# One layer of a hybrid streaming encoder on one core: four joint stores in the tail, halved last casts, and the places of four other steps

## The chip, the cores and the metric

The kernel runs on one core of one Trainium2 chip. The core's engines are TensorE (PE in the profile, its weight loads apart as PEld), VectorE (DVE), ScalarE (ACT), GpSimd (POOL) and SyncE (SP). Each runs its own list of instructions in order and waits for the others by semaphores. DMAs are issued from an engine's list and are carried out beside it. The metric is the device time of one execution in microseconds (us).

## The reference

The input `x` is 512 tokens by 2048 channels, everything is float32. One layer computes two branches from the same normalised input, merges them, and adds a gated embedding:

```python
h = rmsnorm(x, g_pre)
qkv, z_a, b_raw, a_raw, glu_in, z_b, gate_logits = split(h @ w_in)
# A: short convolution, 16 heads of 128, chunks of 64 tokens, a gated delta rule
#    with a triangular solve in each chunk and a state carried over the chunks
o_a = rmsnorm(gated_delta_chunked(q, k, v, g_log, beta), g_dn_out) * silu(z_a)
y_a = o_a @ w_br_a
# B: gated linear unit, depthwise convolution of 31 taps, layer norm
u = silu(layernorm(depthwise(glu(glu_in)) + b_dw)) * silu(z_b)
y_b = u @ w_br_b
mixed = (gate_a * y_a + gate_b * y_b) @ w_out
x = x + rmsnorm(mixed, g_post)
e = p @ w_ple_proj                                  # 256 channels to 2048
x = x + rmsnorm(sigmoid(x @ w_ple_gate) * e, g_ple)
```

`rmsnorm` divides by the root of a mean over all 2048 channels of a token, so the last line needs a token's whole row of gate products before any of it can be scaled.

## The kernel before, in words

**Products.** Every float32 product is made of three TensorE products: both operands are split into a high part (a cast, on ScalarE) and a low part (the difference, on VectorE or GpSimd), and high by high, high by low and low by high are added up in PSUM. A piece of weights is 128 by 1024; its load (SP), its cast and its subtraction run ahead of TensorE by a few pieces. The usual product is 128 by 128 by 512.

**Order of work.** Python code issues the work in one order; a scheduler then orders each engine's list by a model of when inputs are ready, with the issue order as priority. `pin` (keep_in_program_order) keeps an instruction behind the one that was issued before it on its engine. Side work is written as generators: `spawn` starts one, every big product calls `tick`, and a generator that yields n continues n ticks later. `finish` runs what is left without any products in between.

**Start.** `load_x` loads and normalises the four token tiles and, between them, computes the embedding `e`: `embed` (L221) runs for each of four column blocks j, with four PSUM banks (`e_ps`, out of six), one a token tile. For each half k of the 256 channels and each token tile it issues high by high (L228), high by low weights (L229) and low by high (L230). The results are copied (`e_sb`) by ScalarE and VectorE in turn and stored to `pe_dram` by POOL (L507).

**Heads.** The products by `w_in` (L183 to L187) follow; `group(g)`, eight of them with two heads each, runs among them by ticks. A group transposes k, q and v, computes the Gram products `pg` (L862) of all chunks and a product with a swap matrix that exchanges the halves of the squared norms (L869, `pe`), then solves the triangular systems: 31 steps on VectorE (L898, L899), one after the other, each followed by a yield of as many ticks as its size times `pace`, 2.6. The last transpose of the result (`Tc`, L913) is followed by a yield of 22 ticks and by the products `py` and `pz` (L919, L922) and `pd` (L934). Then two `head_scan` run over the chunks, ending in a norm, a product with z and four transposes (`po`, L797). The last group, g = 7, has no group behind it: its scans end in `finish("heads")`.

**Middle.** Branch B, the two products by `w_br_a` and `w_br_b`, and `w_out` follow. `presums` lets POOL's DMAs add up blocks of weights in DRAM, for products that use seven block products in the place of eight; its queue work lies beside the heads.

**End.** The gate product is made of 14 block products (`PLAN`): P1, P2, P3, P6, P7, Q4, Q5 for two column blocks jp. LOW are token tiles 0 and 1, HIGH are 2 and 3. `next_piece_sw` (L1620) keeps up to four split pieces ahead: `split_piece` (L1602) casts a whole piece, 1024 wide, into a buffer of `ring` or `s3` (L1616) and subtracts (L1617). There are 112 pieces in all; the last four, 108 to 111, are those of the last block product, Q4 of jp 1. After each piece's products `step` (L1905) issues up to three `chores` and up to two `scalings`. Chores of a finished product add blocks (L1960), take a sigmoid (L1950), multiply by e and square (L1951, L1953), and multiply by the gain (L1956).

`with_x` (L1723) forms x1, x plus the normalised branch output. For LOW it also stores x1 to the output (L1727), since for these tiles the last sum is made in DRAM: when LOW's gated embedding is complete, `final_steps` (L1967) takes the mean of squares (L1574, L1575) and its power of -1/2 (POOL, L1577), and for each column block j scales on ScalarE (L1973) and adds to the output with an accumulating DMA of POOL (L1974). Eight such DMAs go out, 256 KB each, 128 rows of 2 KB. For HIGH the last sum is one VectorE instruction (L1976) and a plain store by SP (L1977).

After the last product come, in the order of issue: the third tile's mean and power, the additions for the fourth tile in two halves (L2045), the third's first final step, then the fourth's sigmoid and products alternating with the third's steps, the fourth's mean and power, and the rest of the final steps.

Of the kernel before, what the change touches and what calls it, by code (L numbers as in the profile page):

```python
# [81 lines left out]
def _body(ctx, tc, A, out):  # L82
# [138 lines left out]
    def embed(j, pT, xps):  # L221
        ps = [xps.tile([P, T], F32, tag="xp", name="e_ps") for _ in range(NTT)]
        for k in range(2):
            wh, wl = prepped.popleft()
            lh, ll = pT[k]
            for tt in range(NTT):
                b = slice(tt * P, (tt + 1) * P)
                mm(ps[tt], lh[:, b], wh, start=k == 0, stop=False)  # L228
                mm(ps[tt], lh[:, b], wl, start=False, stop=False)  # L229
                mm(ps[tt], ll[:, b], wh, start=False, stop=k == 1)  # L230
        for tt in range(NTT):
            e = slots.tile([P, T], F32, tag="s", name="e_sb")
            (nc.vector.tensor_copy if tt % 2 else nc.scalar.copy)(e, ps[tt])
            e_sb[j, tt] = e
# [572 lines left out]
    def group(g):  # L807
# [48 lines left out]
        for hh, h, s4, kq, kc, vc in heads:  # L856
            pg = wps.tile([P, NTT, 2, 64], F32, tag="w", name="pg")
            for c in range(8):
                tt, par = divmod(c, 2)
                a = 64 * par  # L860
                pair = kq[:, tt, 0:2, :] if par == 0 else kq[:, tt, 3:1:-1, :]
                mm(pg[a:a + 64, tt, :, :], kq[:, tt, 3 * par, :], pair, start=True, stop=True)  # L862
            pgs.append(pg)
        yield 6
# [3 lines left out]
        pe = wps.tile([P, T], F32, tag="w", name="pe")  # L868
        mm(pe[:, 0:8], cc(C_SWAP), sq, start=True, stop=True)  # L869
# [21 lines left out]
        owed, pace = 0.0, 2.6  # L891
# [22 lines left out]
        yield 22  # L914
# [686 lines left out]

    def split_piece():  # L1602
# [3 lines left out]
        two = []  # L1606
        for m in range(2):
# [12 lines left out]
    def next_piece_sw():  # L1620
        while entries and len(sources) < (3 if entries[0][0] is GATE else 5):
            load(*entries.popleft())
        while len(pieces) < (3 if count[0] < 10 else 4) and sources:
            split_piece()
            if entries and len(sources) < (3 if entries[0][0] is GATE else 5):
                load(*entries.popleft())
        return pieces.popleft()

    def mms(ps, pr, piece, q, t, opnd=None):
        wh, wl = piece  # L1630
        for n in range(2):
            kk = 2 * q + n
            c = slice(n * T, n * T + T)
            lh, ll = (opnd or mix_opnd)(OPND[pr], kk, t)
            mm(ps, lh, wh[:, c], start=kk == 0, stop=False)  # L1635
            mm(ps, ll, wh[:, c], start=False, stop=False)  # L1636
            mm(ps, lh, wl[:, c], start=False, stop=kk == 7)  # L1637
# [82 lines left out]
    def x_steps(tts, xr):  # L1720
        rm = inv_rms(ssm[:, tts[0]:tts[0] + 2, :], f"m{tts[0]}")

        def with_x(j):  # L1723
            for n, tt in enumerate(tts):
                pin(nc.vector.scalar_tensor_tensor(x1[tt][j], x1[tt][j], rm[:, n:n + 1], xr.pop((tt, j)), ALU.mult, ALU.add))
                if tt in LOW:
                    nc.gpsimd.dma_start(rows(out, tt, j), x1[tt][j])  # L1727
# [177 lines left out]
    def step():  # L1905
# [5 lines left out]
        for _ in range(2):  # L1911
            if scalings:
                scalings.popleft()()
# [16 lines left out]
    e_t = {}  # L1930
    grow = [None] * 4

    def load_e(tts, j, home=None):
        if home:
            two = [unit(home, "e") for _ in tts]
        else:
            w = s3.tile([P, 1024], F32, tag="rw", name="ew", bufs=5)
            two = [w[:, 0:T], w[:, T:]]
        for tt, e in zip(tts, two):
# [27 lines left out]
    def final_steps(tt, width=4):  # L1967
        rp = inv_rms(ssp[:, tt:tt + 1, 0:width], f"p{tt}")

        def one(j):  # L1970
            e = e_t[tt, j]
            if tt in LOW:
                pin(nc.scalar.activation(e, e, AF.Copy, scale=rp))  # L1973
                pin(nc.gpsimd.dma_start(rows(out, tt, j), e, accum_op=ALU.add))  # L1974
                return
            pin(nc.vector.scalar_tensor_tensor(e, e, rp, x1[tt][j], ALU.mult, ALU.add))  # L1976
            nc.sync.dma_start(rows(out, tt, j), e)  # L1977
        return [lambda j=j: one(j) for j in range(4)]

    v = {}  # L1980
    for pr, jp in PLAN[:-1]:
# [25 lines left out]
        elif pr == "P3":  # L2007
# [4 lines left out]
            if jp:  # L2012
                chores.append(lambda: scalings.extend(final_steps(0) + final_steps(1)))
# [28 lines left out]
    third = final_steps(2)  # L2042
    for h in range(2):
        cs = slice(h * 256, h * 256 + 256)
        pin(nc.vector.tensor_tensor(u[1][:, cs], ps[1][:, cs], u[1][:, cs], ALU.add))  # L2045
    third[0]()
    for h in range(2):
        halves_[h][0]()
        third[1 + h]()
    for h in range(2):  # L2050
        halves_[h][1]()
    fourth = final_steps(3, 5)
    third[3]()
    for f in fourth:
        f()
# [65 lines left out]
```

## Time and profile before

| | |
|---|---|
| time, median of 3 runs | 2391.76 us (2390.85 to 2392.19) |
| profiled execution | 2392.39 us |
| its span | 2390.6 us |
| TensorE busy in it | 2366.1 us |
| VectorE busy | 1905.8 us |
| ScalarE busy | 1235.1 us |
| GpSimd busy | 560.4 us |
| TensorE's granted clock, mean | 0.998 of full speed |

Times within the profile count from the start of the span. A row of the timeline has the start, the duration (of several instructions together where xN stands behind), the engine, the line of the kernel, the operation, the tiles out<-in with their shape, and in brackets the idle time of the engine before it and what ended it. An engine followed by q (SPq) is its sequencer. A row of waits has who waited for whom, the total in us, how often, and the longest. A row of windows has the stretch, its length, then for PE, PEld, DVE, ACT and POOL the busy time with the number of instructions in brackets, the granted clock, the DMA share and GB/s. A row "DMA to landing" has the shortest, the median and the longest time from issue to the last byte.

### The profile page before, as it was taken

What the parts mean: (1) busy time and instruction counts of PE and PEld (TensorE: products, weight loads), DVE (VectorE), ACT (ScalarE), POOL (GpSimd) and SP (SyncE); (2) the same over time, 40 slices, a digit from 0 to 9 for tenths busy, and PEclk for the clock granted to TensorE, in tenths of its full rate; (3) what the DMA queues carried; (4) which work ended last, traced back from release to release, by engine and by line L of the source; (5) the groups of instructions that cost most, each with busy time, mean ns of one, the idle gap of its engine ahead of it and who ended that gap; (6) DMA issues with size and microseconds to landing.
All of it is one profiled execution on the core that took longest, in us unless ns stands there. A gap on an engine that the chain in (4) does not pass through costs nothing.

```text
span 2390.6 us, 33765 instructions
## 1 busy us (share of the span) xinstructions
PE 2366.1 (99%) x11774; PEld 1949.3 (82%) x11774; DVE 1905.8 (80%) x3509; ACT 1235.1 (52%) x2413; POOL 560.4 (23%) x607
## 2 busy tenths in 40 slices
PE   9999999999999999999999999999999999999997
PEld 7888888887888888888888887888888888888786
DVE  8878888776777786767778677999998898887877
ACT  6455455555644545454544544554423665665655
POOL 1001100011122122231321231798861000000001
PEclk9999999999999999999999999999999999999999
DMA  7577766765486768686874884443353577767666
GB/s 277 164 202 200 200 204 197 205 180 188 146 224 173 209 200 252 175 228 194 220 239 144 214 237 115 148 150 106 115 167 119 186 249 240 258 221 234 214 229 167
DMA packets 152827, 465.67 MB, mean 195 GB/s; under 512 B 17872, under 2 KB 26320, under 8 KB 151120
## 3 DMA queue, kind: packets, MB, share of 16 engines
q1 hardware_dynamic: 121456, 334.00, 41.2%
q0 software_dynamic: 28896, 125.32, 22.6%
q10 hardware_dynamic: 2304, 4.20, 0.6%
q8 instruction: 92, 1.51, 0.3%
q14 instruction: 79, 0.65, 0.1%
HBM read 426.22 MB, written 134.22 MB: 234 GB/s over the span
## 4 chain that ended last, share of the span: by engine, by line
PE 88%; DVE 4%; issue 3%; DMA 2%; ACT 2%; POOL 0%; SPq 0%; POOLq 0%; DVEq 0%; ACTq 0%
PE g L185 13%; PE g L187 13%; PE g L183 13%; PE zp L471 6%; PE zp L473 6%; PE zp L472 6%; PE f L1637 4%; PE f L1636 4%; PE f L1635 4%; PE yp L1466 2%; PE yp L1462 2%; PE yp L1464 2%; PE yp L1143 2%; PE yp L1141 2%; PE yp L1139 2%
## 5 line engine op out<-in xcount | busy, mean ns | idle before, releaser
L185 PE MATMUL g<-hl,w 128*128 128x512 f32 x1536 | 610.5, 397 | 0.0
L187 PE MATMUL g<-hh,w 128*128 128x512 f32 x1536 | 608.3, 396 | 0.0
L183 PE MATMUL g<-hh,w 128*128 128x512 f32 x1536 | 608.1, 396 | 0.0
L126 ACT CAST w<-raw 128x512 fp32r<-128x512 f32 x564 | 345.8, 617 | 416.1 <-PE g L187 240.6
L127 DVE TENSOR_TENSOR w<-raw,w 128x512 fp32r<-128x512 f32 x450 | 310.4, 696 | 85.5 <-ACT w L126 83.1
L185 PEld LDWEIGHTS g<-hl,w 128*128 128x128 f32 x1536 | 289.0, 188 | 55.2 <-issue 1.4
L187 PEld LDWEIGHTS g<-hh,w 128*128 128x128 f32 x1536 | 289.1, 188 | 54.1 <-POOL w L127 0.3
L183 PEld LDWEIGHTS g<-hh,w 128*128 128x128 f32 x1536 | 289.1, 188 | 54.0
L1011 DVE SCALAR_TENSOR_TENSOR uc<-up,vec,uc 128x497 f32<-128x497 f32 (+29 forms) x390 | 282.3, 733 | 13.2 <-ACT uc L990 1.9
L127 POOL TENSOR_TENSOR w<-raw,w 128x512 fp32r<-128x512 f32 x114 | 146.5, 1299 | 57.2 <-ACT w L126 55.1
L1635 PE MATMUL f<-wsp,oph 128*128 128x512 f32 x352 | 137.8, 391 | 0.0
L710 DVE SCALAR_TENSOR_TENSOR cv<-g,vec,cv 128x511 f32<-128x511 f32 x144 | 106.6, 740 | 39.1 <-ACT cv L708 38.8
L1636 PE MATMUL f<-wsp,opl 128*128 128x512 f32 x352 | 137.4, 390 | 0.0
L1637 PE MATMUL f<-wsp,oph 128*128 128x512 f32 x352 | 137.2, 390 | 0.0
L1617 DVE TENSOR_TENSOR wsp<-raw,wsp 128x1024 fp32r<-128x1024 f32 x81 | 98.7, 1222 | 34.5 <-ACT wsp L1616 28.9
L1616 ACT CAST wsp<-raw 128x1024 fp32r<-128x1024 f32 x81 | 83.8, 1047 | 64.1 <-PE f L1636 40.7
L1141 PE MATMUL yp<-w,oh 128*128 128x512 f32 x256 | 100.1, 391 | 0.0
L1143 PE MATMUL yp<-w,ol 128*128 128x512 f32 x256 | 99.5, 391 | 0.0
L1139 PE MATMUL yp<-w,oh 128*128 128x512 f32 x256 | 99.1, 389 | 0.0
L898 DVE TENSOR_TENSOR prod<-UT,VT 128x2 f32<-128x2 f32 (+30 forms) x248 | 87.6, 353 | 6.5
L1033 POOL TENSOR_TENSOR uc<-uc,pr 128x511 f32<-128x511 f32 (+29 forms) x60 | 75.9, 1266 | 8.3 <-ACT pr L1032 7.7
L721 POOL COPY kq<-kc 128x512 f32<-128x512 f32 x16 | 11.5, 720 | 282.9 <-issue 150.9
(438 smaller groups left out, 4947.4 us busy)
## 6 DMA issues: line engine op xcount, KB each, us to landing
raw<-in_w_in SPq DMA_DIRECT2D x194, 512.0 KB, 3.8
wb_sums<-in_w_br_b POOLq DMA_DIRECT2D x48, 512.0 KB, 8.7
wo_sums<-in_w_out POOLq DMA_DIRECT2D x48, 512.0 KB, 9.0
wp_sums<-in_w_ple_gate POOLq DMA_DIRECT2D x48, 512.0 KB, 8.9
raw<-in_w_br_a SPq DMA_DIRECT2D x32, 512.0 KB, 3.3
raw<-wb_sums SPq DMA_DIRECT2D x32, 512.0 KB, 4.4
raw<-wp_sums SPq DMA_DIRECT2D x32, 512.0 KB, 3.4
raw<-in_w_ga SPq DMA_DIRECT2D x24, 512.0 KB, 4.8
```

Source lines behind the costliest of these rows:

```text
L126: nc.scalar.copy(hi, rq)
L127: low_part[0].tensor_tensor(lo, rq, hi.bitcast(F32), ALU.subtract)
L183: mm(ps, wh, rh, start=(k == 0), stop=False)
L185: mm(ps, wh, rl, start=False, stop=False)
L187: mm(ps, wl, rh, start=False, stop=(k == NK - 1))
L1011: pin(nc.vector.scalar_tensor_tensor(y[:, s:], u[:, 0:T - s], vv(w0 + TAPS - 1 - s), y[:, s:], ALU.mult, ALU.add))
L1139: mm(ps[tt], lh[:, b], wh, start=k == 0, stop=False)
L1141: mm(ps[tt], lh[:, b], wl, start=False, stop=False)
L1143: mm(ps[tt], ll[:, b], wh, start=False, stop=k == NK - 1)
L1635: mm(ps, lh, wh[:, c], start=kk == 0, stop=False)
L1636: mm(ps, ll, wh[:, c], start=False, stop=False)
L1637: mm(ps, lh, wl[:, c], start=False, stop=kk == 7)
```

## The change

Six edits:

- `embed`: the products of one half k are issued by weight part. First high by high for the four token tiles, then low by high, then high by low weights.
- `group`: the swap product stands right behind the Gram products, ahead of the pause of six ticks, and takes its PSUM bank from the pool `sps`, no more from `wps`.
- `group`, for g = 7 alone: `pace` 2.3 for 2.6, and the pause ahead of `py` 18 ticks for 22.
- `split_piece`, for pieces 108 to 111: the high and low parts lie in four buffers of 128 by 512 from `hpool`, cast and subtracted half by half; `next_piece_sw` keeps up to six pieces ahead once piece 108 is next.
- x1 of LOW is stored by `step`, one of eight stores in each of the steps 8 to 15, no more by `with_x`. `step` issues one scaling, not two.
- LOW's end: `low_ends` takes both tiles' means and powers, and for each column block scales both tiles and adds them with one accumulating DMA of 512 KB (256 rows of 2 KB). There are four of these in the place of eight. In the tail, the third tile's first final step is issued ahead of the additions for the fourth.

```diff
--- before.py
+++ after.py
@@ -223,11 +223,9 @@
         for k in range(2):
             wh, wl = prepped.popleft()
             lh, ll = pT[k]
-            for tt in range(NTT):
-                b = slice(tt * P, (tt + 1) * P)
-                mm(ps[tt], lh[:, b], wh, start=k == 0, stop=False)
-                mm(ps[tt], lh[:, b], wl, start=False, stop=False)
-                mm(ps[tt], ll[:, b], wh, start=False, stop=k == 1)
+            for n, (l, w) in enumerate(((lh, wh), (ll, wh), (lh, wl))):
+                for tt in range(NTT):
+                    mm(ps[tt], l[:, tt * P:(tt + 1) * P], w, start=k + n == 0, stop=k == 1 and n == 2)
         for tt in range(NTT):
             e = slots.tile([P, T], F32, tag="s", name="e_sb")
             (nc.vector.tensor_copy if tt % 2 else nc.scalar.copy)(e, ps[tt])
@@ -861,12 +859,12 @@
                 pair = kq[:, tt, 0:2, :] if par == 0 else kq[:, tt, 3:1:-1, :]
                 mm(pg[a:a + 64, tt, :, :], kq[:, tt, 3 * par, :], pair, start=True, stop=True)
             pgs.append(pg)
+        pe = sps.tile([P, P], F32, tag="s", name="pe")
+        mm(pe[:, 0:8], cc(C_SWAP), sq, start=True, stop=True)
         yield 6
         for hh, h, s4, kq, kc, vc in heads:
             nc.vector.scalar_tensor_tensor(W[:, s4, 0, :], pgs[hh][:, :, 0, :], -1.0, Ec[:, s4, :], ALU.mult, ALU.mult)
             nc.vector.tensor_tensor(W[:, s4, 1, :], pgs[hh][:, :, 1, :], Ec[:, s4, :], ALU.mult)
-        pe = wps.tile([P, T], F32, tag="w", name="pe")
-        mm(pe[:, 0:8], cc(C_SWAP), sq, start=True, stop=True)
         epsq = hd.tile([P, 8], F32, tag="epsq", name="epsq")
         nc.vector.tensor_scalar(epsq, pe[:, 0:8], EPS, EPS * P, ALU.add, ALU.mult)
         G.update(epsq=epsq, c=c_all)
@@ -888,7 +886,7 @@
         nc.vector.memset(UTf[:, 0:1024:33], 1.0)
         yield
         prod = hd.tile([P, 256], F32, tag="prod", name="prod", bufs=1)
-        owed, pace = 0.0, 2.6
+        owed, pace = 0.0, 2.6 if g < NH // 2 - 1 else 2.3
         for j in range(30, -1, -1):
             n, i0 = 32 - j, j // 4
             ni = 8 - i0
@@ -911,7 +909,7 @@
             dst = VP[r, :, par, b:b + 32]
             nc.scalar.copy(dst.rearrange("p x (i r) -> p x i r", r=4), Vd[r].rearrange("p i r x -> p x i r"))
             nc.vector.transpose(Tc[r, :, b:b + 32], dst)
-        yield 22
+        yield 22 if g < NH // 2 - 1 else 18
         pz = wps.tile([P, 8, 64], F32, tag="w", name="pz")
         py = wps.tile([P, 8, 32], F32, tag="w", name="py")
         for x in range(8):
@@ -1599,11 +1597,21 @@
         nc.sync.dma_start(raw, src[jp, blk, q])
         sources.append(raw)
 
+    LAST = 2 * 56 - 4
+
     def split_piece():
         src = sources.popleft()
         n = count[0]
         count[0] += 1
         two = []
+        if n >= LAST:
+            hi, lo = [[unit((hpool, "h"), "wl", F32R) for _ in range(2)] for _ in range(2)]
+            for m in range(2):
+                rq = src[:, m * T:(m + 1) * T]
+                nc.scalar.copy(hi[m], rq)
+                nc.vector.tensor_tensor(lo[m], rq, hi[m].bitcast(F32), ALU.subtract)
+            pieces.append((hi, lo))
+            return
         for m in range(2):
             if n < 8:
                 two.append(ring.tile([P, 1024], F32R, tag="w", name="wsp") if n % 3 < 2 else
@@ -1620,21 +1628,20 @@
     def next_piece_sw():
         while entries and len(sources) < (3 if entries[0][0] is GATE else 5):
             load(*entries.popleft())
-        while len(pieces) < (3 if count[0] < 10 else 4) and sources:
+        while len(pieces) < (3 if count[0] < 10 else 4 if count[0] < LAST else 6) and sources:
             split_piece()
             if entries and len(sources) < (3 if entries[0][0] is GATE else 5):
                 load(*entries.popleft())
         return pieces.popleft()
 
     def mms(ps, pr, piece, q, t, opnd=None):
-        wh, wl = piece
+        wh, wl = [w if isinstance(w, list) else (w[:, 0:T], w[:, T:]) for w in piece]
         for n in range(2):
             kk = 2 * q + n
-            c = slice(n * T, n * T + T)
             lh, ll = (opnd or mix_opnd)(OPND[pr], kk, t)
-            mm(ps, lh, wh[:, c], start=kk == 0, stop=False)
-            mm(ps, ll, wh[:, c], start=False, stop=False)
-            mm(ps, lh, wl[:, c], start=False, stop=kk == 7)
+            mm(ps, lh, wh[n], start=kk == 0, stop=False)
+            mm(ps, ll, wh[n], start=False, stop=False)
+            mm(ps, lh, wl[n], start=False, stop=kk == 7)
 
     banks = [-1]
 
@@ -1723,8 +1730,6 @@
         def with_x(j):
             for n, tt in enumerate(tts):
                 pin(nc.vector.scalar_tensor_tensor(x1[tt][j], x1[tt][j], rm[:, n:n + 1], xr.pop((tt, j)), ALU.mult, ALU.add))
-                if tt in LOW:
-                    nc.gpsimd.dma_start(rows(out, tt, j), x1[tt][j])
 
         def turn(k2, ps):
             for n in range(4):
@@ -1908,9 +1913,11 @@
         for _ in range(2 if passed[0] < 20 else 3):
             if chores:
                 chores.popleft()()
-        for _ in range(2):
-            if scalings:
-                scalings.popleft()()
+        if scalings:
+            scalings.popleft()()
+        if 8 <= passed[0] < 16:
+            tt, j = divmod(passed[0] - 8, 4)
+            nc.gpsimd.dma_start(rows(out, tt, j), x1[tt][j])
 
     pair = [-1]
 
@@ -1928,6 +1935,7 @@
         return ps
 
     e_t = {}
+    e_low = {}
     grow = [None] * 4
 
     def load_e(tts, j, home=None):
@@ -1936,6 +1944,7 @@
         else:
             w = s3.tile([P, 1024], F32, tag="rw", name="ew", bufs=5)
             two = [w[:, 0:T], w[:, T:]]
+            e_low[j] = w
         for tt, e in zip(tts, two):
             e_t[tt, j] = e
             nc.sync.dma_start(e, pe_dram[j, tt])
@@ -1969,13 +1978,19 @@
 
         def one(j):
             e = e_t[tt, j]
-            if tt in LOW:
-                pin(nc.scalar.activation(e, e, AF.Copy, scale=rp))
-                pin(nc.gpsimd.dma_start(rows(out, tt, j), e, accum_op=ALU.add))
-                return
             pin(nc.vector.scalar_tensor_tensor(e, e, rp, x1[tt][j], ALU.mult, ALU.add))
             nc.sync.dma_start(rows(out, tt, j), e)
         return [lambda j=j: one(j) for j in range(4)]
+
+    def low_ends():
+        rp = [inv_rms(ssp[:, tt:tt + 1, 0:4], f"p{tt}") for tt in LOW]
+
+        def one(j):
+            for tt in LOW:
+                pin(nc.scalar.activation(e_t[tt, j], e_t[tt, j], AF.Copy, scale=rp[tt]))
+            pin(nc.gpsimd.dma_start(out[0:2 * P, j * T:(j + 1) * T].rearrange("(t p) c -> p t c", p=P),
+                                    e_low[j].rearrange("p (t c) -> p t c", t=2), accum_op=ALU.add))
+        scalings.extend(lambda j=j: one(j) for j in range(4))
 
     v = {}
     for pr, jp in PLAN[:-1]:
@@ -2010,7 +2025,7 @@
                 chores.append(chore_tt(d[t], ps[t], d[t], ALU.add))
             gated_out(LOW, 2 * jp + 1, d)
             if jp:
-                chores.append(lambda: scalings.extend(final_steps(0) + final_steps(1)))
+                chores.append(low_ends)
         elif pr == "P7":
             u, s5 = v["P1", jp], v["Q5", jp]
             for t in range(2):
@@ -2040,18 +2055,17 @@
         scalings.popleft()()
     halves_ = [gate_steps(3, 2, u[1], h) for h in range(2)]
     third = final_steps(2)
+    third[0]()
     for h in range(2):
         cs = slice(h * 256, h * 256 + 256)
         pin(nc.vector.tensor_tensor(u[1][:, cs], ps[1][:, cs], u[1][:, cs], ALU.add))
-    third[0]()
-    for h in range(2):
-        halves_[h][0]()
-        third[1 + h]()
-    for h in range(2):
-        halves_[h][1]()
+    third[1]()
+    for n in range(2):
+        for h in range(2):
+            halves_[h][n]()
+    third[2]()
     fourth = final_steps(3, 5)
-    third[3]()
-    for f in fourth:
+    for f in third[3:] + fourth:
         f()
 
 
```

## The prediction

> **What bounds the kernel now.** I read the page first (span, share of each engine), then TensorE's waits, then the timeline of the last 40 us engine by engine.
>
> ```profile
> span 2390.6 us, 33765 instructions
> PE 2366.1 (99%) x11774; PEld 1949.3 (82%) x11774; DVE 1905.8 (80%) x3509; ACT 1235.1 (52%) x2413; POOL 560.4 (23%) x607
> ...
> PE tp L1732 <- DVE snap L1725: 1.8, 1, 1.8
> PE po L797 <- DVE O L793: 1.6, 2, 0.8
> ...
> 2374.57 0.39 PE L1637 MATMUL f<-wsp,oph 128*128 128x512 f32 x1
> ```
>
> TensorE is busy for 99%. What it loses is 2390.6 - 2366.1 = 24.5 us, and of that 2390.6 - 2374.96 = 15.6 us is the tail after its last product. So an edit saves time if it takes instructions or a wait off TensorE (the two waits shown are the largest in the middle), or if it shortens the tail. The tail:
>
> ```profile
> 2363.38 2.73 POOL L1974 DMA_DIRECT2D out_dram<-ew  x3 [0.66 <-ACT ew L1973]
> 2369.22 0.87 POOL L1974 DMA_DIRECT2D out_dram<-ew  x1 [3.11 <-issue]
> 2370.53 0.86 POOL L1974 DMA_DIRECT2D out_dram<-ew  x1 [0.44 <-ACT snap L1950]
> 2371.85 0.86 POOL L1974 DMA_DIRECT2D out_dram<-ew  x1 [0.47 <-ACT snap L1953]
> 2374.85 0.87 POOL L1974 DMA_DIRECT2D out_dram<-ew  x1 [2.14 <-issue]
> 2377.84 0.87 POOL L1974 DMA_DIRECT2D out_dram<-ew  x1 [2.12 <-ACT snap L1950]
> 2378.41 0.89 POOL L1577 TENSOR_TENSOR rmsp<-totp,mhalf_c 128x1 f32<-128x1 f32 x1
> 2383.09 0.99 POOL L1577 TENSOR_TENSOR rmsp<-totp,mhalf_c 128x1 f32<-128x1 f32 x1 [3.79 <-DVE totp L1575]
> ...
> 2375.84 0.15 DVE L1575 TENSOR_SCALAR totp<-totp 128x1 f32<-128x1 f32 x1
> 2375.92 0.74 DVE L2045 TENSOR_TENSOR snap<-f,snap 128x256 f32<-128x256 f32 x2
> 2379.33 0.75 DVE L1976 SCALAR_TENSOR_TENSOR e<-e,rmsp,snap 128x512 f32<-128x512 f32 x1 [2.67 <-POOL rmsp L1577]
> 2386.10 0.75 DVE L1976 SCALAR_TENSOR_TENSOR e<-e,rmsp,snap 128x512 f32<-128x512 f32 x1
> ```
>
> The third token tile's power of -1/2 (POOL, 2378.41) had its input at 2375.99. It ran 2.4 us later because POOL issues in order and stood at the eighth accumulating store until 2377.84. VectorE waited 2.67 us for it, and the end follows 2390.6 - 2378.41 = 12.2 us after it. The first question is therefore when POOL gets through its stores.
>
> **The joint stores.** Their pace is set by a limit on what POOL may have in flight.
>
> ```profile
> L1974 POOL DMA_DIRECT2D out_dram<-ew x8: 856/873/1447, 2363.4 to 2377.8; - x8
> DMA to landing us min/median/max: 4.4/5.9/7.0
> ...
> L507 POOL DMA_DIRECT2D pe_dram<-e_sb x16: 539/548/966, 27.2 to 38.6; - x16
> DMA to landing us min/median/max: 2.7/5.6/7.4
> ```
>
> Three accumulates go out back to back (2363.38, 2.73 long for all three). Then POOL stands until 2369.22, 5.8 after the first one, which is what one takes to land (5.9). The next two follow 1.31 us apart, as I read it with the landings of the second and third, and then it stands again. So three of these are in flight, never four. Plain stores of the same 256 KB (L507) are issued 11.4 / 15 = 0.76 us apart at 5.6 us to land, so about seven of them are in flight: an accumulate takes about twice the room of a plain store. A joint store has 256 rows of 2 KB where a single one has 128. If room goes by rows, two joint stores are four singles, which did not fit: one joint store in flight. That is the step on which my forecast rests.
>
> Price of one joint store from issue to landing: a single takes at least 4.4, and in a run of them each further 256 KB adds 1.31; 4.4 + 1.31 = 5.7. The ends are 4.4 (a second half that is free) and 7.0 (the slowest single) + 1.31 = 8.3. I take 6.2, between the sum and the median 5.9 + 1.31 = 7.2, nearer to the sum because no other store of POOL competes; with an allowance of 0.3 until POOL has issued the next, 6.5 per store. The Trainium skill (DMA: Bandwidth & Descriptors, Anatomy of one DMA — SWDGE (gpsimd) path) fits such a transfer as 2.0 us fixed plus bytes over 436 GB/s, as an estimate 2.6 us for 256 KB and 3.2 us for 512 KB; the trace disagrees for accumulates, whose smallest is 4.4. By that rule, with the same allowance, the fourth would go out 3 x 3.5 us after the first, and the change would not be slower (rival 2).
>
> **When the first joint store goes out.**
>
> ```profile
> raw<-wp_sums SPq DMA_DIRECT2D x32, 512.0 KB, 3.4
> L127 DVE TENSOR_TENSOR w<-raw,w 128x512 fp32r<-128x512 f32 x450 | 310.4, 696 | 85.5 <-ACT w L126 83.1
> ...
> 2352.63 6.08 SPq L1599 DMA_DIRECT2D raw<-wp_sums  x3
> ...
> 2354.21 1.28 DVE L1960 TENSOR_TENSOR d<-f,d 128x512 f32<-128x512 f32 x2
> 2357.13 1.23 DVE L1617 TENSOR_TENSOR wsp<-raw,wsp 128x1024 fp32r<-128x1024 f32 x1 [0.84 <-ACT wsp L1616]
> 2361.22 0.21 DVE L1574 TENSOR_REDUCE totp<-ssp 128x1 f32<-128x4 f32 x2
> 2365.76 1.23 DVE L1617 TENSOR_TENSOR wsp<-raw,wsp 128x1024 fp32r<-128x1024 f32 x1 [2.28 <-ACT wsp L1616]
> 2366.90 1.28 DVE L1960 TENSOR_TENSOR snap<-f,snap 128x512 f32<-128x512 f32 x2
> ...
> 2362.22 2.56 ACT L1973 ACTIVATE ew<-ew,rmsp 128x512 f32<-128x512 f32 x4
> ```
>
> Looking six pieces ahead, the step that split one piece now splits three (107, 108, 109) before the additions of P3 (2354.21) are issued, and VectorE works in order. The load of 109 is issued at 2352.63 and lands 3.4 later, at 2356.0; a cast and two subtractions of a half, 0.7 each, bring 2358.0. There P3's additions start, 3.8 later than before. From them to the sums it took 2361.22 - 2354.21 = 7.0. Of this two subtractions (2357.13 and one more like it, 1.2 each) and a wait of 0.84 now lie ahead of it; without them it is 3.8, but they also hid ScalarE's sigmoids and squares. So the sums come at 2361.8 to 2365.0, taken 2363.2. In the kernel before 2363.38 - 2361.22 = 2.2 lay between sums and store, with one scaling of 0.64 (2.56 / 4); with two, 2.8. First joint store: 2364.6 to 2367.8, taken 2366.0. The halved casts are free otherwise: a half takes 0.70 where a whole piece takes 1.23, 0.17 more a piece, beside the products that run until 2374.96; even without that cover it is 4 x 0.17 = 0.7.
>
> Then POOL: fourth store issued at 2366.0 + 3 x 6.5 = 2385.5, 1.2 for its issue (0.87 for a single, 1.45 the longest), and the third tile's power at 2386.7 (bounds by 4.4 and 8.3 with 0.3: 2381.3 and 2393). The power stands behind the store on POOL because the scaling that feeds the store precedes, on ScalarE, the square that feeds the power.
>
> **The tail's new order.** The third tile's first final step now stands before the additions L2045, with their sigmoid behind. In the kernel before, these (0.74) and the sigmoid lay inside the 2.67 wait; now they follow the power. From additions to the fourth tile's power: 2383.09 - 2375.92 = 7.2, less the wait of 2.67 = 4.5. From that power to the end: 2390.6 - 2383.09 = 7.5. So from the third power on: 0.9 + 0.7 (first final step) + 4.5 + 7.5 = 13.6 where it was 12.2. Behind the waiting step on VectorE stand the additions, both gate products and the fourth tile's sum; ScalarE's sigmoids and squares and POOL's last power wait for those.
>
> **The swap of the squared norms (L869).**
>
> ```profile
> 752.52 0.40 PE L183 MATMUL g<-hh,w 128*128 128x512 f32 x1
> 752.76 0.28 PE L869 MATMUL pe<-sq,cst 128*128 128x8 f32 x2
> 752.90 0.48 PE L185 MATMUL g<-hl,w 128*128 128x512 f32 x1
> 753.21 0.40 PE L187 MATMUL g<-hh,w 128*128 128x512 f32 x1
> ```
>
> From 752.52 to 753.21 lies 0.69 where two big products take 0.46: the swap costs 0.23 a group, alone among big ones. In the run of small Gram products short ones follow each other, and no more than 752.90 - 752.76 = 0.14 of it should stay. Eight groups: 0.09 to 0.23 each, 0.7 to 1.8 in all, taken 1.4. The squares it reads are finished ahead of the Gram products, and its result is read after them, so no wait comes with it.
>
> **The last pair's chain.** The chain's units sum to 56.4 over the 31 steps, so pace 2.3 for 2.6 takes 17 of 146 product slots out, and the pause 4 more: 21 x 0.23 = 4.8 us earlier.
>
> ```profile
> 1405.60:1438.00 32.40, 32.40 (x145) 26.84 (x144) 28.33 (x81) 11.45 (x18) 7.11 (x11) 1.00 0.93 254
> ...
> 1437.52 0.44 DVE L913 STREAM_TRANSPOSE Tc<-VP 32x256 f32<-32x256 f32 x1 [0.26 <-ACT VP L912]
> 1439.14 0.69 PE L919 MATMUL py<-Tc,W 32*32 32x32 f32 x32
> ```
>
> In this stretch VectorE is busy 28.33 of 32.40, 4.1 free, and the result was 1439.14 - 1437.96 = 1.2 ahead of TensorE. Brought forward by 4.8, up to 1 us of new wait can appear there if VectorE does not close its gaps. What can go is the output steps' wait at L797, 1.6, since later work of the pair stands among products again. I take -0.5, bounds -1.6 and +1.0.
>
> **Embedding and the moved stores.**
>
> ```profile
> 17.70 0.19 PEld L229 LDWEIGHTS e_ps<-w,ph 128*128 128x128 f32 x1 [0.47 <-DVE w L280]
> ...
> L1727 POOL DMA_DIRECT2D out_dram<-c x4: 539/550/609, 2197.7 to 2208.9; - x4
> 2223.91 1.61 POOL L1577 TENSOR_TENSOR rmsm<-totm,mhalf_c 128x2 f32<-128x2 f32 x1 [11.88 <-DVE totm L1575]
> ```
>
> Grouping by weight part puts the low part last, so the 0.47 wait can go; but all four banks then end together, their copies bunch, and the next bank may come one copy late, 0.7 by L127's row for a tile of that size: -0.3 to +0.7, taken 0. The stores of x1 leave the stretch around 2200 for steps 8 to 15, some 50 us later; POOL had been idle for 11.88 before 2223.91, so neither place makes the 1.8 wait at L1732, and I cost it at 0. The cover is POOL's idle time; without it, it is 8 x 0.55 = 4.4 of POOL.
>
> **Sum.** Power at 2386.7, less the 1.4 + 0.5 saved earlier, 13.6 to the end: 2398.4 of span. The profiled execution took 2392.39, 1.8 more than its span and 0.6 more than the median 2391.76: 2400.2.
>
> **Rivals.** (1) Two or more joint stores in flight. For it: I know the room only as between three and four singles. The Trainium skill (DMA: Bandwidth & Descriptors, The descriptor swizzle) counts one closing descriptor per transfer beside the data, so two joint ones would take a little less than four singles; no run here shows it. POOL is then free when the sum is ready, and P7's additions, before held at 2366.90 by the subtraction of 2365.76 and its 2.28 wait, come about 2 earlier, so the first final step is done near the last product's end at 2374.96; additions at 2375.1 and 4.5 + 7.5 from there: 2387.1, less 1.9, plus 1.8: 2387.0. If P7 comes no earlier, it is 2376.0 + 13.6 - 1.9 + 1.8 = 2389.5; with nothing saved earlier either, 2391.4; with the swap and the heads at their best, 2385.5. What decides is the second joint store: issued within 2 us of the first, this rival holds. (2) One in flight, but the joint store is hardly longer than a single one: 4.7 per store, power at 2381.3, and 2381.3 + 13.6 - 1.9 + 1.8 = 2394.8. Against it: the issues at 2369.22, 2370.53 and 2371.85 are 1.31 apart, so 256 KB more are not free. With the estimate from the Trainium skill's page above (DMA: Bandwidth & Descriptors, Anatomy of one DMA — SWDGE (gpsimd) path), 3.5 per store, it would be 2391.2. (3) POOL's order puts the power before the fourth store: 2366.0 + 13.0 + 1.2 = 2380.2 and 2393.7. That is also how the change would fail to do what it says. Against it: the order of ScalarE above.
>
> **How the numbers follow.** Forecast 0.47 (own range 2395 to 2405, by the power at 2381.3 to 2392), rival 1 0.32, rival 2 0.11, rival 3 0.10. No change means within 0.2%, 4.8 us, about what a measurement can tell: 2387.0 to 2396.5. Slower: 0.45 + 0.01 + 0.02 = 0.48. Faster: 0.17 of rival 1, its lower half. Same: 0.02 + 0.15 + 0.10 + 0.08 = 0.35. The range 2385 to 2404 leaves out the forecast's upper end and little of rival 1, about 0.1 to 0.15.
>
> **What would show it.** Right: joint stores on POOL more than 5 us apart, each shortly after the landing of the one before; the third power more than 5 us after its sum; VectorE waiting there longer than 2.67. Wrong: two joint stores issued within 2 us, or a third power within 1 us of its sum. L869 should stand between L862's products, and the wait at L797 shrink.

## The result and the profile after

The changed kernel takes 2407.35 us (median of 6 runs, 2404.93 to 2410.42) where the kernel before, timed beside it, takes 2391.59 (2390.18 to 2393.69). The ratio is 1.0066, with an interval of 1.0053 to 1.0079: slower by 15.8 us. The forecast said slower, at 2400.2, which is 8.6 above the kernel before, and its range ended at 2404.0. The profiled execution took 2404.93, the shortest of the six, where the one of the kernel before took 2392.39, so the traces explain 12.5 us of the loss; the other 3.3 us have no trace.

The page of the changed kernel, first lines:

```profile
span 2403.2 us, 33766 instructions
PE 2365.9 (98%) x11774; PEld 1947.9 (81%) x11774; DVE 1906.0 (79%) x3513; ACT 1236.3 (51%) x2417; POOL 557.7 (23%) x603
```

TensorE is as busy as before (2365.9 and 2366.1). All of the loss in the profiled execution is idle time of TensorE. Line numbers here and below are those of each kernel's own file, so the same line of code can have another number than before. TensorE's last product, in the timeline:

```profile
2376.66 0.39 PE L1644 MATMUL f<-wl,oph 128*128 128x512 f32 x1
```

Before, this product started at 2374.57. So 2.1 us are lost ahead of the tail; the rest, 2403.2 - 2376.66 = 26.5 against 2390.6 - 2374.57 = 16.0, or 10.5 us, is lost in the tail. The tail on POOL, then on VectorE and ScalarE:

```profile
2369.54 1.27 POOL L1991 DMA_DIRECT2D out_dram<-ew  x1 [1.34 <-ACT ew L1990]
2375.99 1.23 POOL L1991 DMA_DIRECT2D out_dram<-ew  x1 [5.18 <-ACT ew L1990]
2382.47 1.21 POOL L1991 DMA_DIRECT2D out_dram<-ew  x1 [5.25 <-issue]
2389.01 1.21 POOL L1991 DMA_DIRECT2D out_dram<-ew  x1 [5.33 <-issue]
2389.74 1.07 POOL L1575 TENSOR_TENSOR rmsp<-totp,mhalf_c 128x1 f32<-128x1 f32 x1
...
2372.05 1.29 DVE L1960 TENSOR_TENSOR e<-snap,e 128x512 f32<-128x512 f32 x2 [2.56 <-ACT snap L1959]
...
2378.41 0.15 DVE L1573 TENSOR_SCALAR totp<-totp 128x1 f32<-128x1 f32 x1
...
2390.85 0.75 DVE L1981 SCALAR_TENSOR_TENSOR e<-e,rmsp,snap 128x512 f32<-128x512 f32 x1 [12.29 <-POOL rmsp L1575]
...
2367.70 3.79 ACT L1990 ACTIVATE ew<-ew,rmsp 128x512 f32<-128x512 f32 x6 [2.02 <-POOL rmsp L1575]
...
out_dram<-ew POOLq DMA_DIRECT2D x4, 512.0 KB, 6.1
```

The joint stores go out 6.45, 6.48 and 6.54 us apart. The last row is of the list of DMA issues: the median from issue to landing is 6.1, so each store is issued 0.3 to 0.4 after the one before it has landed. The third tile's sum is ready at 2378.56 and its power runs at 2389.74, behind the fourth store. VectorE waits 12.29 us where it waited 2.67. A trap for the reader: the bracket behind the store of 2375.99 names ScalarE's scaling, but the six scalings in that row were over by 2371.5. A wait for several things is put down to one of them; here it was the landing of the store before, 6.1 after 2369.54.

The waits of TensorE in the changed kernel (who waited for whom, total us, times, longest):

```profile
PE yp L1464 <- DVE w L127: 2.1, 2, 1.8
PE po L795 <- DVE O L791: 1.7, 2, 1.2
...
PE e_ps L228 <- DVE e_sb L231: 0.7, 3, 0.3
PE yp L1137 <- ACT lsq L1202: 0.7, 1, 0.7
```

The two waits of `yp` have no counterpart before. The first stands in the products by `w_br_b`, which the diff does not touch. The wait for `O`, which the last pair's edit was to shorten, did not shrink (L795 here, L797 before: 1.7 and 1.6). Set beside the same products of the kernel before, TensorE is 0.9 us behind at 60 us, 0.3 at 1326, 0.5 ahead at 1545, 3.4 behind at 1957, and 2.1 behind from 2240 to the end.

### The profile page after: what moved, and what is told of

It is laid out like the page before. It is cut to its first block, busy times and chain, and to the rows that moved or that the text cites. A ratio compares the mean times of both kernels' runs of the same rounds, so it can differ in the third digit from the quotient of the medians.

```text
span 2403.2 us, 33766 instructions
## 1 busy us (share of the span) xinstructions
PE 2365.9 (98%) x11774; PEld 1947.9 (81%) x11774; DVE 1906.0 (79%) x3513; ACT 1236.3 (51%) x2417; POOL 557.7 (23%) x603
## 4 chain that ended last, share of the span: by engine, by line
PE 86%; DVE 5%; issue 3%; DMA 3%; ACT 2%; POOL 1%; SPq 0%; POOLq 0%; DVEq 0%; ACTq 0%
PE g L185 13%; PE g L187 13%; PE g L183 13%; PE zp L469 6%; PE zp L471 6%; PE zp L470 6%; PE f L1644 4%; PE f L1643 4%; PE f L1642 4%; PE yp L1464 2%; PE yp L1462 2%; PE yp L1460 2%; PE yp L1141 2%; PE yp L1139 2%; PE yp L1137 2%
## 5 line engine op out<-in xcount | busy, mean ns | idle before, releaser
L1009 DVE SCALAR_TENSOR_TENSOR uc<-up,vec,uc 128x511 f32<-128x511 f32 (+29 forms) x390 | 285.2, 734 | 13.2 <-ACT uc L988 0.7
L1642 PE MATMUL f<-wsp,oph 128*128 128x512 f32 x336 | 131.6, 392 | 0.0
L1643 PE MATMUL f<-wsp,opl 128*128 128x512 f32 x336 | 131.2, 390 | 0.0
L1644 PE MATMUL f<-wsp,oph 128*128 128x512 f32 x336 | 131.0, 390 | 0.0
L1625 DVE TENSOR_TENSOR wsp<-raw,wsp 128x1024 fp32r<-128x1024 f32 x77 | 93.8, 1221 | 29.8 <-ACT wsp L1624 24.2
```

The source lines that it names most:

```text
L1009: pin(nc.vector.scalar_tensor_tensor(y[:, s:], u[:, 0:T - s], vv(w0 + TAPS - 1 - s), y[:, s:], ALU.mult, ALU.add))
L1642: mm(ps, lh, wh[n], start=kk == 0, stop=False)
L1643: mm(ps, ll, wh[n], start=False, stop=False)
L1644: mm(ps, lh, wl[n], start=False, stop=kk == 7)
```

## The experiments

The theory: one joint store is in flight at a time, since room in POOL's DMA queue goes by rows, and POOL's in-order queue carries this to the third tile's power. Rivals: room or pace by bytes; the loss from the casts, from the heads, or from the transfers themselves. Each time stands beside runs of the kernel before on the same chip; these took 2392.88 (e1 to e4) and 2393.05 (e5 to e8), some 1.4 us more than the 2391.6 from which the expected times count. Several times came out above the expected ones by about that, and the differences are the better measure. The kernels described as "as e1" start from the first one:

**The tail's edits alone (e1).** The embedding, the swap and the pace are as before, all else as changed.

```diff
-            for n, (l, w) in enumerate(((lh, wh), (ll, wh), (lh, wl))):
...
-        pe = sps.tile([P, P], F32, tag="s", name="pe")
...
-        owed, pace = 0.0, 2.6 if g < NH // 2 - 1 else 2.3
+        owed, pace = 0.0, 2.6
...
-        yield 22 if g < NH // 2 - 1 else 18
+        yield 22
```

> The change without its embedding, swap and last-pair edits: halved casts, moved x1 stores, joint stores and the tail's new order alone. Theory (one joint store in flight, POOL's power behind the fourth): stores 6.5 us apart, the third tile's power within 1 us of the fourth store's issue and over 8 us after its sum, VectorE waiting over 9 us for it, 13.5 us from that power to the end; 2401 to 2403 us where the kernel before has 2391.6. Rival (the other three edits are what costs): within 2 us of the kernel before.

Measured: 2402.94 us where the kernel before has 2392.88, ratio 1.0043 (1.0028 to 1.0058). POOL and VectorE:

```profile
2366.94 1.27 POOL L1993 DMA_DIRECT2D out_dram<-ew  x1 [1.34 <-ACT ew L1992]
2373.44 1.23 POOL L1993 DMA_DIRECT2D out_dram<-ew  x1 [5.23 <-ACT ew L1992]
...
2386.37 1.21 POOL L1993 DMA_DIRECT2D out_dram<-ew  x1 [5.13 <-issue]
2387.10 1.07 POOL L1577 TENSOR_TENSOR rmsp<-totp,mhalf_c 128x1 f32<-128x1 f32 x1
...
2357.52 1.28 DVE L1971 TENSOR_TENSOR d<-f,d 128x512 f32<-128x512 f32 x2
...
2364.10 0.21 DVE L1574 TENSOR_REDUCE totp<-ssp 128x1 f32<-128x4 f32 x2
...
2388.21 0.75 DVE L1983 SCALAR_TENSOR_TENSOR e<-e,rmsp,snap 128x512 f32<-128x512 f32 x1 [12.24 <-POOL rmsp L1577]
```

The tail alone makes 10 of the 16 us. The last three rows are VectorE's: P3's additions, the sums of LOW, and the wait for the third tile's power.

**Single stores (e2).**

```diff
-            for tt in LOW:
-                pin(nc.scalar.activation(e_t[tt, j], ...))
-            pin(nc.gpsimd.dma_start(out[0:2 * P, ...], e_low[j] ..., accum_op=ALU.add))
+            for tt in LOW:
+                pin(nc.scalar.activation(e_t[tt, j], ...))
+                pin(nc.gpsimd.dma_start(rows(out, tt, j), e_t[tt, j], accum_op=ALU.add))
```

> As e1_tail, with eight single accumulating stores of 128 rows in the place of four joint ones of 256. Theory (room by rows, three singles in flight): groups of three, eighth issued 14 to 15 us after the first as in the kernel before, the power behind it about 5 us earlier than in e1_tail, 2396 to 2398 us. Rival (bytes through POOL's queue set the pace, joint or not): same as e1_tail within 1 us.

Measured: 2396.84 us, ratio 1.0016 (1.0007 to 1.0026). The eighth store follows the first by 2384.32 - 2370.07 = 14.3 in its trace. Same bytes, same rows, and 6 us less than joint: a transfer of 256 rows seems to leave no room for part of the next, which the next run tests. The profiled execution took 2399.91, 3.1 more than the median, and TensorE's granted clock in it was 0.97 from 2180 to 2240 us where the kernel before has 1.00; so only differences within this trace are used.

```profile
2370.07 2.73 POOL L1993 DMA_DIRECT2D out_dram<-ew  x3 [0.66 <-ACT ew L1992]
2375.18 0.87 POOL L1993 DMA_DIRECT2D out_dram<-ew  x1 [2.38 <-ACT snap L1964]
...
2384.32 0.87 POOL L1993 DMA_DIRECT2D out_dram<-ew  x1 [2.19 <-issue]
```

**Joint over columns (e3).** The two halves of `ew` hold two column blocks of one tile, no more two tiles of one block:

```diff
...
-            pin(nc.gpsimd.dma_start(out[0:2 * P, j * T:(j + 1) * T] ..., e_low[j] ..., accum_op=ALU.add))
+            pin(nc.gpsimd.dma_start(out[tt * P:(tt + 1) * P, jp * 1024:(jp + 1) * 1024], e_low[tt, jp], accum_op=ALU.add, max_dma_last_dim=4096))
```

> As e1_tail, but each of the four stores of 512 KB holds one token tile and two column blocks: 128 rows of 4 KB, not 256 rows of 2 KB. Theory (room goes by rows): three in flight, fourth issued when the first has landed, 6 to 9 us after it, so that POOL is free when the third tile's sum is ready; power within 1 us of its sum, 2388 to 2391 us. Rival (room goes by bytes, or one transfer of 512 KB at a time): stores 6 to 7 us apart as in e1_tail, 2400 us and more.

Measured: 2392.49 us, ratio 0.9998 (0.9989 to 1.0008), the profiled execution 2390.85.

```profile
2366.93 0.92 POOL L1998 DMA_DIRECT2D out_dram<-ew  x1 [1.28 <-ACT ew L1997]
2368.17 0.87 POOL L1998 DMA_DIRECT2D out_dram<-ew  x1 [0.31 <-issue]
2369.38 0.87 POOL L1998 DMA_DIRECT2D out_dram<-ew  x1 [0.35 <-issue]
2373.43 0.87 POOL L1998 DMA_DIRECT2D out_dram<-ew  x1 [3.18 <-ACT ew L1997]
2376.10 0.56 POOL L1577 TENSOR_TENSOR rmsp<-totp,mhalf_c 128x1 f32<-128x1 f32 x1 [1.80 <-DVE totp L1575]
```

This separates rows from bytes. The store is as large as the joint one (512 KB) and there are four of them, but three are in flight (issued within 2.5 us, a median of 7.6 to land), and POOL is idle when the power's input comes. The 10 us are gone. The median is above the expected 2388 to 2391: against the kernel before on its chip it is 0.4 faster, where at least 0.6 was expected. That no more than three fit is not shown by this run: the fourth store's scaling ended at 2372.80, only 0.3 before the first store landed at 2373.12.

**Whole casts (e4).** As e1, with no piece halved and four kept ahead:

```diff
-    LAST = 2 * 56 - 4
+    LAST = 2 * 56
```

> As e1_tail, with the last four pieces cast whole and four pieces ahead as in the kernel before, not halved and six ahead. Theory (the halved casts put P3's additions behind three pieces' subtractions and the late load of piece 109): first joint store 3 to 4 us earlier, at about 2363.5 to 2364 in the trace, stores still 6.5 us apart, so everything behind it 3 to 4 us earlier: 2398 to 2399 us. Rival (the first store is late for another reason, such as both tiles' scalings): under 1 us earlier.

Measured: 2400.32 us, ratio 1.0032 (1.0020 to 1.0043), 2.6 us less than e1.

```profile
2364.61 1.27 POOL L1993 DMA_DIRECT2D out_dram<-ew  x1 [1.34 <-ACT ew L1992]
...
2354.76 1.28 DVE L1971 TENSOR_TENSOR d<-f,d 128x512 f32<-128x512 f32 x2
```

P3's additions start at 2354.76 where e1 has 2357.52, and the first joint store at 2364.61 where e1 has 2366.94, though TensorE ran 0.9 later in this trace than in e1's. So the halved casts, with six pieces ahead, cost about 3 us through VectorE's order. In time the gain of 2.6 is a little less than the 3 to 4 expected, and the rival falls.

**The pace alone (e5).** The kernel before with the two lines of the last pair:

```diff
-        owed, pace = 0.0, 2.6
+        owed, pace = 0.0, 2.6 if g < NH // 2 - 1 else 2.3
...
-        yield 22
+        yield 22 if g < NH // 2 - 1 else 18
```

> The kernel before with the last pair's pace 2.3 and pause of 18 alone. Theory (the pace moves the scheduler's model, and VectorE's order in the later products by w_br_b with it): TensorE 0.5 to 0.8 us ahead after the heads, then 2.5 to 3.5 us lost around 1920 to 1935 in waits for L127's subtractions, as in the changed kernel: 2393 to 2395 us. Rival (those waits are a matter of one run or of the start's delay): TensorE 0.5 to 0.8 ahead to the end, 0.5 us faster than before.

Measured: 2395.69 us, ratio 1.0015 (1.0006 to 1.0024). TensorE's waits, and VectorE in that stage:

```profile
PE yp L1466 <- DVE w L127: 2.2, 3, 1.7
...
1925.28 2.09 DVE L1273 TENSOR_TENSOR usf<-ur 128x256 f32<-128x256 f32 x6
1927.29 1.28 DVE L1282 TENSOR_TENSOR opl<-usf,oph 128x512 fp32r<-128x512 f32 x2
1928.50 0.75 DVE L1273 TENSOR_TENSOR usf<-ur 128x256 f32<-128x256 f32 x2
1929.17 0.68 DVE L127 TENSOR_TENSOR w<-raw,w 128x512 fp32r<-128x512 f32 x1
```

The time is 2.6 more than the kernel before on its chip. The same product, set beside the kernel before: 0.4 us ahead at 1326, 0.4 ahead at 1545 (behind the heads), 3.4 behind at 1957. The lead of 0.4 is there before the last pair's chain begins, at about 1405, so in this trace the edit gains nothing at its own place. Two numbers of the heads move VectorE's order 400 us later: eight sums and differences (L1273) and two subtractions for operands stand ahead of the weights' subtraction (1929.17) for which TensorE waits 1.7 us. The changed kernel's wait of 0.7 for `lsq` is in this trace too. In the kernel before, VectorE does at the same place:

```profile
1924.25 1.29 DVE L127 TENSOR_TENSOR w<-raw,w 128x512 fp32r<-128x512 f32 x2
1925.45 0.69 DVE L1234 TENSOR_TENSOR ur<-ur,zb 128x512 f32<-128x512 f32 x1
1926.06 1.29 DVE L127 TENSOR_TENSOR w<-raw,w 128x512 fp32r<-128x512 f32 x2
```

VectorE's instruction list in that stage is the same in the changed kernel and in this one. The lists with the embedding, the swap or the tail alone are those of before. Why the scheduler's model turns on the pace stays open.

**Embedding and swap alone (e6).** The kernel before with these lines in the place of its own (the added ones alone are shown):

```diff
+            for n, (l, w) in enumerate(((lh, wh), (ll, wh), (lh, wl))):
+                for tt in range(NTT):
+                    mm(ps[tt], l[:, tt * P:(tt + 1) * P], w, start=k + n == 0, stop=k == 1 and n == 2)
...
             pgs.append(pg)
+        pe = sps.tile([P, P], F32, tag="s", name="pe")
+        mm(pe[:, 0:8], cc(C_SWAP), sq, start=True, stop=True)
         yield 6
```

> The kernel before with the embedding's products by weight part and the swap behind the Gram products alone. Theory: the embedding costs 0.8 to 1.0 us at the start, all of it by 60 us; the swap still costs 0.23 to 0.24 us of TensorE in each group, so between the groups nothing is saved: 0.9 us slower than before, within what the runs can tell. Rival (the forecast's: the swap saves 0.1 to 0.2 a group): TensorE's lag of 0.9 shrinks by 1.4 over the eight groups and ends as a lead of 0.5.

Measured: 2394.61 us beside 2393.05, ratio 1.0005 (0.9997 to 1.0014): no difference that can be told. The swap in its trace:

```profile
749.78 0.40 PE L183 MATMUL g<-hh,w 128*128 128x512 f32 x1
750.11 1.97 PE L860 MATMUL pg<-kq 128*64 128x128 f32 x32
752.01 0.39 PE L863 MATMUL pe<-sq,cst 128*128 128x8 f32 x2
752.25 0.47 PE L185 MATMUL g<-hl,w 128*128 128x512 f32 x1
```

From the swap to the next big product lie 752.25 - 752.01 = 0.24 us, as among big ones, and the lag behind the kernel before is 0.73 at 771 and 0.73 at 1326, with five groups between. The swap is no cheaper there. The embedding is not settled: new waits of 0.7 for `e_sb` are in this trace and in the changed kernel's, and both lag by 0.9 at 60 us, but kernels with the old embedding lag there by 0.1 to 1.1 too (e5 0.1, e1 0.4, e2 1.1).

**The power ahead of the later stores (e7).** As e1:

```diff
-        if scalings:
+        if len(scalings) > 2:
             scalings.popleft()()
...
-    while scalings:
-        scalings.popleft()()
...
+    scalings.popleft()()
     third[2]()
     fourth = final_steps(3, 5)
+    scalings.popleft()()
```

`step` leaves two joint stores over; they are issued behind the third tile's gate products and behind the fourth's power.

> As e1_tail, but the third and the fourth joint store are issued behind the third tile's power and the fourth tile's power. Theory (the loss is POOL's order: the power behind stores of which only one is in flight): power within 1 us of its sum, VectorE's last steps end near 2385, and the end is then set by the fourth joint store's landing, 4 x 6.5 us after the first at 2367: 2393 to 2396 us. Rival (joint transfers themselves slow the rest down): 2400 us and more.

Measured: 2397.6 us, ratio 1.0020 (1.0011 to 1.0029), 1.6 above the expected range; the profiled execution 2396.42.

```profile
2374.41 0.56 POOL L1577 TENSOR_TENSOR rmsp<-totp,mhalf_c 128x1 f32<-128x1 f32 x1 [0.28 <-DVE totp L1575]
2380.01 1.22 POOL L1993 DMA_DIRECT2D out_dram<-ew  x1 [5.04 <-ACT ew L1992]
...
2387.31 1.22 POOL L1993 DMA_DIRECT2D out_dram<-ew  x1 [5.47 <-issue]
```

The power runs with its sum, VectorE's last step ends at 2384.6, and the span of 2394.6 ends with the fourth store. So the power's place costs about half of the tail's loss (4.6 us over the kernel before are left of e1's 10.1), and four joint stores after one another are too long in this order too.

**Columns, with the old casts and the old tail order (e8).** As e3, with the tail's instructions in the order of the kernel before and:

```diff
-    LAST = 2 * 56 - 4
+    LAST = 2 * 56
...
-    third[0]()
     for h in range(2):
         cs = slice(h * 256, h * 256 + 256)
         pin(nc.vector.tensor_tensor(u[1][:, cs], ps[1][:, cs], u[1][:, cs], ALU.add))
+    third[0]()
...
```

> The kernel before with the moved x1 stores and four stores of one token tile and two column blocks (128 rows of 4 KB), whole casts and the tail's old order (additions ahead of the third tile's first final step). Theory (POOL free when the sum is ready, and the old order keeps the additions off the power's path): additions start at their sum as before, no 2.67 us wait behind them, 12.0 us from the additions to the end: about 2388 in the span, 2 to 3.5 us faster than before. Rival (the transfers' landing or the fourth tile's chain ends last anyway): within 1 us of before.

Measured: 2390.22 us beside 2393.05, ratio 0.9990 (0.9981 to 0.9998): 2.8 us faster than the kernel before in the medians, as expected, with an interval of 0.5 to 4.5 by the ratio. POOL and VectorE:

```profile
2372.86 0.87 POOL L1998 DMA_DIRECT2D out_dram<-ew  x1 [4.93 <-ACT ew L1997]
2375.74 0.56 POOL L1577 TENSOR_TENSOR rmsp<-totp,mhalf_c 128x1 f32<-128x1 f32 x1 [2.02 <-DVE totp L1575]
...
2375.58 0.74 DVE L2066 TENSOR_TENSOR snap<-f,snap 128x256 f32<-128x256 f32 x2
2376.34 0.75 DVE L1988 SCALAR_TENSOR_TENSOR e<-e,rmsp,snap 128x512 f32<-128x512 f32 x1
```

The additions fill the time of the power, no wait is left, and the end is 2387.6 - 2375.58 = 12.0 after them. The old casts and the old order came in together, so what each is worth is not separated. Here the fourth store waited for its scaling, which ended at 2372.43, and with it only two stores were in flight.

**Half stores (e9).** As e2, each store cut in two of 64 rows:

```diff
-                pin(nc.gpsimd.dma_start(rows(out, tt, j), e_t[tt, j], accum_op=ALU.add))
+                for r in (slice(0, 64), slice(64, P)):
+                    pin(nc.gpsimd.dma_start(rows(out, tt, j)[r], e_t[tt, j][r], accum_op=ALU.add))
```

> As e2_single, with each accumulating store cut in two of 64 rows of 2 KB (128 KB): sixteen stores. Theory (room goes by rows, between 384 and 511 of an accumulating store's): the first six or seven issues follow without standing, under 1 us apart, then about one per landing. Rival (three accumulating stores at a time, whatever their size, or room by bytes with 512 KB of columns counting three): the fourth issue stands some 4 us behind the third, as in e2_single.

Measured: one run, 2397.98 us, so its time says little; its trace does. The first eight issues start within 4.0 us. From the ninth on each starts 0.2 to 0.4 after a landing, and with it seven are in flight, never eight.

```profile
2369.18 12.05 POOL L1994 DMA_DIRECT2D out_dram<-ew  x14 [0.64 <-ACT ew L1992]
2381.54 1.67 POOL L1994 DMA_DIRECT2D out_dram<-ew  x2 [0.31 <-issue]
...
DMA to landing us min/median/max: 3.2/5.8/8.0
```

## Why the prediction was wrong

**Right: what bounds the tail.** One joint store in flight, 6.5 us per store (measured 6.49 on average), the power behind the fourth, and 13.6 from the power to the end (measured 2403.2 - 2389.74 = 13.5). The trace itself puts rival 1 (two joint stores in flight) and rival 2 (a joint store as short as a single one) out: stores 6.5 apart, each landing 6.1 after its issue. e3 and e9 show the step behind it, that room goes by rows. Rival 3 was not the order that was built; e7 made one like it, and it fell short for a reason the rival did not have: it let the end follow the power, while the fourth store's landing ended later.

**Wrong: the lead of 1.9 us ahead of the tail.** "Power at 2386.7, less the 1.4 + 0.5 saved earlier": instead TensorE came 2.1 later. That is 4.0 of the 4.7 us between the sum and the profiled execution, and it is the step that failed. The size is of one trace: in e2 and e9, whose kernels are e1's up to the tail's last stores, TensorE's last product came 2.9 and 2.5 later than before. But there TensorE was busy for longer (2368.4 and 2368.2 us), where in the changed kernel the 2.1 are waits, and e5's median, 2.6 over the kernel before, bears out that the pace costs that much. The two terms of the lead failed for different reasons.

- The swap, "taken 1.4", is worth nothing. I let the swap become cheap among small products, but in the run of Gram products it stands last, and its step to the next big product is the same 0.24.
- The last pair, "I take -0.5, bounds -1.6 and +1.0", shows no gain at its place that holds from trace to trace (from 1326 to 1545 us TensorE gained 0.8 in the changed kernel, nothing in e5, and the wait at L797 did not shrink). In a stage that I never looked at it then lost 3.8 by 1957, and in time 2.6 (e5). I took the edit to act where it stands. With a scheduler that orders every engine's list from a model of the whole program, that is an assumption, and it needs bounds of its own.

The embedding, taken as 0, is 0.9 behind at 60 us in both kernels that have its edit, but e6 does not settle it, as said there.

**Mis-sized: the head of the tail.** The first joint store was put at 2366.0, and stands at 2369.54 - 2.1 = 2367.4 on the old count, inside the bounds given. P3's additions started as put (2358.0; 2357.5 in e1, whose TensorE ran 0.4 ahead of the kernel before). From them to the sums I took 5.2 us; e1 has 2364.10 - 2357.52 = 6.6: four half subtractions of 0.7 for the pieces after 109 come in between. That the halved casts delay the first store is shown by e4, where P3's additions start 2.8 earlier; from them to the sums e4 takes as long as the kernel before (7.0), so this part is not the casts' cost, and the mistake was to go too far towards 3.8, the time with such subtractions gone. The power came 0.7 behind the last issue's start where I took 1.2, which gives 0.5 back.

**Half right: P7's additions come earlier.** They start at 2367.01, which is 2.0 earlier on the old count, but the six scalings in a row (ScalarE, 3.79) now stand ahead of the sigmoids, VectorE waits 2.56 for them, and the third tile's sum is no earlier for it. A stall was traded for another one.

**The moved x1 stores** were costed at nothing. TensorE's wait at that place is 0.6 us in the changed kernel and 1.0 to 2.0 in the experiments with the move, 1.4 to 1.8 without; single traces don't settle it.

**The range** took its width from the tail alone. Even with every earlier term at its recorded worst it did not hold the pace's 3.1 us in the trace, and 2.4 us more stay unexplained between the profiled execution and the median. The sum, 2400.2, is one of a profiled execution: it names the 0.6 by which that stood above the median and does not take it off. The Trainium skill's estimate (DMA: Bandwidth & Descriptors, Anatomy of one DMA — SWDGE (gpsimd) path) of 3.2 us for 512 KB does not hold for these accumulates: a joint store alone in flight took 6.1 us from issue to landing.

## What to carry to other kernels

Join DMAs of POOL's queue along their rows' length, not by adding rows: the same 512 KB as 128 rows of 4 KB kept three in flight, as 256 rows of 2 KB one, and that was worth 10 us here (e1 and e3). Before a small instruction is left behind a store on an engine that works in order, ask how long the store may stand for room, and compare that with when the instruction's input is ready. And when a scheduler orders the whole program, compare the instruction lists of stages that an edit does not touch before calling the edit local.

## What the runs showed that was not expected

In flight at most, by rows of an accumulating store: seven of 64 rows (e9), three of 128 (e2; e3 has three too, with rows of twice the length), one of 256 (e1); and seven plain stores of 128 rows in the kernel before. A count of rows/8 + 1 for an accumulate and rows/16 + 1 for a plain store, with room for 64, fits all of these (7 x 9 = 63, 3 x 17 = 51 and 4 x 17 = 68, 33 and 66, 7 x 9 = 63). It is a fit, not shown as such: without the +1, and with room for 56 to 63, the counts fit as well. The Trainium skill (DMA: Bandwidth & Descriptors, The descriptor swizzle) counts nine write descriptors on each of 16 engines for a transfer to 128 partitions, eight of data and a closing one. The traces agree: from 2361 us on POOL's queue moves 1152 packets for the eight stores of the kernel before, 8 x 16 x 9, and 576 for the four of e3. What room a closing one takes is not shown. The joint store's pattern also has one dimension more, its two tiles; no run separates that from its 256 rows, but from 64 to 128 rows (e9 and e2) the pattern is the same and the number in flight falls from seven to three.

A product of 128 by 8 with a full weight load takes the same 0.23 to 0.24 us of TensorE's time, two passes in all, behind a run of small products (e6) as among products of 512 columns (the kernel before).
